# Down projections that keep sums of weights on chip, load the residual, and normalise half of the tokens around the seventh Strassen product

## The chip, the core and the metric

The kernel runs on one core of one Trainium2 chip. The core has five engines with a queue of their own each: TensorE (PE in the profile, its weight loads PEld), VectorE (DVE), ScalarE (ACT), GpSimd (POOL) and SyncE (SP). Here SP only issues DMA transfers, and so does POOL nearly always; 16 DMA engines carry them. The metric is the time of one execution on the device in microseconds (us), lower is better; a median over several runs is compared.

## What is computed

One step of a one-layer hybrid decoder for T = 1032 tokens (1024 of a prompt and 8 samples), D = 1024, all in fp32. Cut to what matters:

```
y1 = layer_norm(ALPHA * x  + 0.5 * swiglu(x,  w1_1, w3_1, w2_1))    # "ffn 1"
y2 = layer_norm(ALPHA * y1 + hybrid_mixer(y1, ...))
y  = layer_norm(ALPHA * y2 + 0.5 * swiglu(y2, w1_2, w3_2, w2_2))    # "ffn 2"

def swiglu(x, w1, w3, w2):
    return (silu(x @ w1) * (x @ w3)) @ w2        # D -> D_FF = 2816 -> D
```

The change touches only the last product of each swiglu, `@ w2`, the normalisation behind it, and the order of the first projections of the mixer behind ffn 1.

## The kernel before

Everything is held transposed: a tile is 128 features by tokens. D is 8 tiles (KD = 8, index m for outputs), D_FF is 22 (index f). Each fp32 matmul is made of three matmuls of a faster 32-bit type: an operand is split into a high part, made by ScalarE (`wh`, `gh`, `XH`), and a low part, raw minus high, made by VectorE (`wl`, `gl`, `XL`), and high x high, low x high and high x low are added up in PSUM (`mm3`, line 172). So every weight block and every operand costs a pass of ScalarE (line 91) and one of VectorE (line 94) before TensorE can use it.

**The up part** (`ffna`) makes g = -silu(x w1) (x w3) for f = 0 to 20 and stores it to DRAM: single tiles in `gs`, and for the 16 tiles f = 3 to 18 ("paired") seven operands of a Strassen scheme, `gt[P1]` to `gt[P7]`, 8 tiles of 516 tokens each (TH_ = 516 is half of the tokens, TQ = 258 a quarter; a third is 344, written `ts(t)`, NT = 3).

**The down part** (`ffnb`) has four stages:
1. `gplain(21)` computes the last tile of g on the spot, in thirds of the tokens, and leaves it split on chip. Meanwhile tile 0 is loaded back (`gload`), and VectorE rebuilds the residual `ACC = XH + XL`, 8 adds of 1032 columns. The input's tiles XH and XL are free from here on, and become the landing place of Strassen operands.
2. *Head units.* For each m and each third t, `unit` multiplies the tiles f = 0 and 21 by their weights (6 matmuls of 344 columns) and VectorE adds the result, scaled, to `ACC[:, m]`. `fill(P1, 0, m)` loads one operand tile of the first product through one of two landing buffers (`gr`) and splits it into XH and XL.
3. *Seven products* in the order P1, P5, P6, P2, P7, P4, P3. Each has four steps mp, each step two groups of 24 matmuls of 258 columns: 192 matmuls. While product o runs, the operands of product o + 1 are filled into the other slot: XH and XL hold two slots. `blocks` fetches the weight blocks of a step. P1, P2 and P4 use one block of w2 (through `wraw`, 3 buffers). P5 needs a sum of two blocks of w2, P6 that sum plus a third, P3 that one plus a fourth, P7 a sum of its own. The parts land in two halves of `rw` (4 buffers), are added on VectorE, and the running sum of P5 and P6 is stored to DRAM (`sd`, issued by POOL) and loaded again for the next product that needs it. VectorE adds PSUM into ACC, with a helper tile U for P1, P6 and P7.
4. *End units.* The tiles f = 1, 2, 19 and 20 are loaded from `gs`, and units of 12 matmuls with weights split beforehand (DRAM `hv`, fetched on POOL's queue) run chunk by chunk: three thirds in ffn 1, four quarters in ffn 2. The layer norm of a chunk (`LN`: total by a matmul with ones, line 214, mean, squares, total of squares, scale, and a new XH and XL) is a generator, `fin`, of steps set between the units of the next chunk. The last chunk's norm in ffn 1 goes on during the first projections of the mixer (`kq`, `ab`), in ffn 2 it is the tail of the kernel, with the output's stores.

The code is written in program order, and a scheduler orders the instructions on each engine; every engine then runs its own in order, and waits at semaphores. SP issues transfers in order too: one that waits for a free buffer holds up those behind it. The lines that move the sums:

```
P5: (a(1, 0), a(1, 1), 0), P6: (sd[0][mp, q], a(0, 0), 1),
P7: (a(0, 0), a(1, 0), None), P3: (sd[1][mp, q], a(0, 1), None)}[i]
...
if z is not None:
    G.dma_start(sd[z][mp, q], two[:, 0])
```

## Time and profile before

| what | value |
|---|---|
| median of 3 runs | 2562.27 us (2559.83 to 2570.35) |
| the profiled execution's own time | 2558.2 us |
| its span on the core | 2556.4 us |
| mean granted clock of TensorE | 0.991 |
| first down part: head units, products, end units | 460.53, 489.11, 658.37 to 707.70 us |
| second down part: head units, products, end units, tail | 2293.32, 2317.59, 2485.27, 2534.10 to 2556.40 us |

The stretches are cut where the first matmul of a stage starts. A row of a stretch gives its length, the busy time of each engine with the number of instructions, the granted clock, the share of the DMA engines and the traffic. Two things are read from it: a stretch with the same matmuls as another but a greater length has waits of TensorE in it (or a lower clock), and an engine whose busy time nears the length has no room for more. Which wait it was is read from the waits by engine, and what stood before it from the timeline.

### The profile page before, as it was taken

Reading aid. Unit: us, or ns where it says so; the run is one execution under the profiler, and the core shown is the slowest. Engines: PE = TensorE matmul, PEld = TensorE weight load, DVE = VectorE, ACT = ScalarE, POOL = GpSimd, SP = SyncE. Lnnn points to the kernel's source line nnn. Section 1 sums busy time; section 2 is a strip of 40 time slices with the busy share of each in tenths; the row PEclk is TensorE's granted clock in tenths of the full one; section 3 lists DMA queues with packets and bytes.
Section 4 is the critical chain, followed back from the end, with each engine's and each line's share of the span. In section 5 each row is a group of like instructions: output and inputs, shape, how many; then the busy total and the mean of one; then the engine's idle time right before and its main releaser. Section 6 shows DMA issues by size and latency. Waiting matters only on the chain.

```text
span 2556.4 us, 48972 instructions
## 1 busy us (share of the span) xinstructions
PE 2486.4 (97%) x18758; PEld 2438.4 (95%) x18758; DVE 1831.2 (72%) x3951; ACT 1168.8 (46%) x2486; POOL 435.2 (17%) x747
## 2 busy tenths in 40 slices
PE   8999999999999999999999999998999999999997
PEld 8999999999988999999999999998999999999996
DVE  7777777676797677777777686764676677777767
ACT  5433333333363746565554647633543333334336
POOL 2112121000102112111111121132521211110010
PEclk9999999999999999999999999999999999999999
DMA  6556555687411111111112111156855645447772
GB/s 231 158 178 192 166 179 167 192 269 228 117 38 54 36 48 45 39 51 34 57 35 58 35 51 37 54 159 166 231 170 146 171 137 144 133 149 228 250 208 67
DMA packets 211306, 326.43 MB, mean 128 GB/s; under 512 B 42544, under 2 KB 82992, under 8 KB 211072
## 3 DMA queue, kind: packets, MB, share of 16 engines
q1 hardware_dynamic: 143456, 192.00, 24.2%
q0 software_dynamic: 56784, 125.24, 16.8%
q10 hardware_dynamic: 10832, 6.07, 0.9%
q8 instruction: 147, 2.41, 0.4%
q14 instruction: 87, 0.71, 0.1%
HBM read 237.05 MB, written 86.18 MB: 126 GB/s over the span
## 4 chain that ended last, share of the span: by engine, by line
PE 48%; issue 20%; DMA 11%; DVE 8%; ACT 8%; POOL 5%; SPq 0%; POOLq 0%; ACTq 0%; DVEq 0%
PE ps_mm L172 29%; PE ps_g L172 5%; DMA gr<-gt 4%; ACT L91 2%; PE ps_g L1022 2%; PE ps_g L337 2%; PE ps_mm L337 2%; PE ps_sq L337 2%; DMA rw<-w 2%; POOL hv L142 2%; PE ps_sq L908 2%; DVE wl L94 1%; PE ps_g L914 1%; PE ps_g L908 1%; DMA s_S<-s 1%
## 5 line engine op out<-in xcount | busy, mean ns | idle before, releaser
L172 PE MATMUL ps_mm<-XH,wh 128*128 128x344 f32 (+1 forms) x2104 | 683.5, 325 | 5.8 <-ACT wh L91 5.7
L172 PE MATMUL ps_mm<-XH,wl 128*128 128x344 f32 (+1 forms) x2104 | 658.8, 313 | 2.0 <-DVE wl L94 2.0
L172 PE MATMUL ps_mm<-XL,wh 128*128 128x344 f32 (+1 forms) x2104 | 658.9, 313 | 0.1
L172 PEld LDWEIGHTS ps_mm<-XH,wh 128*128 128x128 f32 x2104 | 398.1, 189 | 9.6 <-ACT wh L91 5.7
L172 PEld LDWEIGHTS ps_mm<-XH,wl 128*128 128x128 f32 x2104 | 397.9, 189 | 2.8 <-DVE wl L94 2.5
L172 PEld LDWEIGHTS ps_mm<-XL,wh 128*128 128x128 f32 x2104 | 398.8, 190 | 1.7 <-DVE XL L94 0.6
L91 ACT ACTIVATE wh<-wraw 128x512 fp32r<-128x512 f32 (+1 forms) x324 | 197.8, 615 | 237.8 <-PE ps_mm L172 66.5
L94 DVE TENSOR_TENSOR wl<-wraw,wh 128x512 fp32r<-128x512 f32 (+1 forms) x324 | 218.2, 676 | 70.4 <-ACT wh L91 38.8
L337 PE MATMUL ps_g<-CH,wh 128*128 128x258 f32 x740 | 209.6, 283 | 0.6 <-DVE u L94 0.4
L337 PE MATMUL ps_g<-CH,wl 128*128 128x258 f32 x740 | 208.9, 282 | 0.0
L337 PE MATMUL ps_g<-CL,wh 128*128 128x258 f32 x740 | 208.7, 282 | 0.0
L172 PE MATMUL ps_g<-XH,wl 128*128 128x258 f32 (+1 forms) x592 | 175.1, 296 | 9.5 <-DVE wl L94 6.8
L172 PE MATMUL ps_g<-XH,wh 128*128 128x258 f32 (+1 forms) x592 | 173.1, 292 | 2.3 <-ACT wh L91 2.1
L172 PE MATMUL ps_g<-XL,wh 128*128 128x258 f32 (+1 forms) x592 | 172.5, 291 | 0.0
L337 PE MATMUL ps_mm<-XH,wl 128*128 128x258 f32 x592 | 167.0, 282 | 1.2 <-DVE wl L94 1.2
L337 PE MATMUL ps_mm<-XH,wh 128*128 128x258 f32 x592 | 167.3, 283 | 0.0
L337 PE MATMUL ps_mm<-XL,wh 128*128 128x258 f32 x592 | 166.8, 282 | 0.0
L91 ACT ACTIVATE wh<-S 128x512 fp32r<-128x512 f32 x148 | 93.1, 629 | 136.2 <-PE ps_sq L337 49.9
L91 ACT ACTIVATE XH<-gr 128x516 fp32r<-128x516 f32 x112 | 70.4, 634 | 172.5 <-DMA gr<-gt 155.9
L91 ACT ACT_TABLE_LOAD x109 | 139.8, 1283 | 6.0 <-issue 2.6
L337 PEld LDWEIGHTS ps_g<-CH,wh 128*128 128x128 f32 x740 | 139.5, 188 | 1.4 <-DVE u L94 1.2
L337 PEld LDWEIGHTS ps_g<-CL,wh 128*128 128x128 f32 x740 | 139.7, 189 | 0.0
(549 smaller groups left out, 6344.0 us busy)
## 6 DMA issues: line engine op xcount, KB each, us to landing
wraw<-w SPq DMA_DIRECT2D x164, 256.0 KB, 3.1
wraw<-w_in SPq DMA_DIRECT2D x128, 256.0 KB, 2.6
gt<-G POOLq DMA_DIRECT2D x112, 258.0 KB, 2.9
gr<-gt SPq DMA_DIRECT2D x112, 258.0 KB, 3.2
rw<-w SPq DMA_DIRECT2D x96, 256.0 KB, 4.2
wr<-w SPq DMA_DIRECT2D x76, 256.0 KB, 2.9
wh<-hv POOLq DMA_DIRECT2D x52, 256.0 KB, 3.9
wl<-hv POOLq DMA_DIRECT2D x52, 256.0 KB, 4.1
```

The lines of the kernel that those rows point to most:

```text
L91: return S.activation(out, in_, f, **kw)
L94: return (eng or V).tensor_tensor(out, a, b, op=op)
L142: G.dma_start(halves[key][i], x)
L172: PE.matmul(p, a, b, start=(n == 0), stop=(n == 3 * nk - 1))
L337: PE.matmul(ps_[c], a[:, k, :], b, start=(start and n == 0), stop=(n == 11), skip_group_check=not start)
L908: x = PE.matmul(ck(p, i), a, b, start=True, stop=True)
L914: x = PE.transpose(ck(p, i), a, IDT)
L1022: pin(PE.matmul(o[r, c, :], a(c), b(c), start=True, stop=True))
```

## The change

- The sums of weights stay on chip. Four tiles `sw` (two blocks of 512 each, in the place of g tiles) are filled with the first block for P5; the second lands in `wraw`, and VectorE adds it in place. P6 and P3 add their block to the same tile. The DRAM tensors `sd`, 16 stores and 16 loads of 256 KB in each down part, are gone. Only P7 still uses `rw`.
- The residual is loaded by 8 transfers of 528 KB from DRAM (`x` in ffn 1, `X2` in ffn 2) on SP's queue in place of 8 adds on VectorE.
- The tiles loaded from `gs` come in thirds, through the landing places s1 and lnq in place of gr, and those of the end units are asked for during P3 and P7 in place of after the last product.
- Head: tile 0 is the first of the two in the sum in place of 21; the units go (0,0), (0,1), (1,0), (1,1), (0,2), (1,2), and then by m; the fill of P1 comes behind its m's last unit. An operand tile j of a slot is now `XH[:, j, slot * 516 : ...]`, so a slot is half of the tokens of every tile.
- The products go P1, P5, P6, P3, P7, P2, P4. P4 adds only to the first half of the tokens. It is now run behind the first chunk (ffn 1) or the first two chunks (ffn 2) of the end units, which are taken from the second half of the tokens, and the norm of the chunk before it is run in steps inside it. The chunks go 2, 0, 1 in ffn 1 and 2, 3, 0, 1 in ffn 2. The weights of m = 6 and 7, which aren't held, are fetched again after P4.
- The mixer's first projections go third 2, 0, 1 in place of 0, 1, 2.

```diff
-HEAD, END = [21, 0], [1, 2, 19, 20]
+HEAD, END = [0, 21], [1, 2, 19, 20]
...
-        sd = [dr.tile([4, 2, 128, 512], F32, name="sd", tag="sd%d%d" % (n, i)) for i in range(2)]
...
             def gload(f):
                 gh, gl = gtiles()
-                for i in range(2):
-                    s = slice(i * TH_, (i + 1) * TH_)
-                    r = landing()
-                    nc.sync.dma_start(r, gs[f][:, s])
-                    split(gh[:, s], gl[:, s], r)
+                for t in range(NT):
+                    r = third(("s1", "lnq")[t % 2])
+                    nc.sync.dma_start(r, gs[f][:, ts(t)])
+                    split(gh[:, ts(t)], gl[:, ts(t)], r)
...
-                s = slice((j % 2) * TH_, (j % 2) * TH_ + TH_)
-                return [x[:, 4 * slot + j // 2, s] for x in (XH, XL)]
+                return [x[:, j, slot * TH_:(slot + 1) * TH_] for x in (XH, XL)]
...
+                if i == P5:
+                    sums.append(up.tile([128, 2, 512], F32, name="sw", tag="u", bufs=8, padded_shape=[128, 2, TH_]))
                 for q in range(2):
...
-                        two = up.tile([128, 2, 512], F32, name="rw", tag="rw", bufs=4)
-                        raw, o = (two[:, e].rearrange("p (k m) -> p k m", m=128) for e in range(2))
-                        nc.sync.dma_start(two[:, 0] if len(x.shape) == 2 else raw, x)
-                        nc.sync.dma_start(o, y)
+                        o = wp.tile([128, 4, 128], F32, name="wraw", tag="wraw", bufs=3)
+                        raw = quad(sums[mp][:, q]) if i in (P5, P6, P3) else o
+                        if i == P5:
+                            nc.sync.dma_start(raw, a(1, 0))
+                    nc.sync.dma_start(o, a(*{P1: (0, 0), P2: (0, 1), P3: (0, 1), P4: (1, 1), P5: (1, 1), P6: (0, 0), P7: (1, 0)}[i]))
+                    if raw is not o:
                         tt(raw, raw, o, OP.add)
-                        if z is not None:
-                            G.dma_start(sd[z][mp, q], two[:, 0])
...
             for m in range(KD):
-                tt(ACC[:, m, :], XH[:, m, :].bitcast(F32), XL[:, m, :].bitcast(F32), OP.add)
+                nc.sync.dma_start(ACC[:, m, :], (A["x"], X2)[n - 1][:, m, :])
             gts = [got[f] for f in HEAD]
-            for m in range(KD):
-                w = wload(w2[m][:, :2], 2)
-                fill(P1, 0, m)
-                for t in range(NT):
-                    unit(m, t, ts(t), w)
+            ws = {}
+            for m, t in [(0, 0), (0, 1), (1, 0), (1, 1), (0, 2), (1, 2)] + [(m, t) for m in range(2, KD) for t in range(NT)]:
+                if t == 0:
+                    ws[m] = wload(w2[m][:, :2], 2)
+                unit(m, t, ts(t), ws[m])
+                if t == NT - 1:
+                    fill(P1, 0, m)
...
-            order = [P1, P5, P6, P2, P7, P4, P3]
+            order = [P1, P5, P6, P3, P7, P2, P4]
...
+                    if order[o + 1:o + 2] in ([P7], [P2]):
+                        if mp % 2:
+                            got.append(gload(END[len(got)]))
+                    yield
...
+            p4 = (n, product(len(order) - 1))
             if n == 1:
-                pending = last_units(lnidx, last, [ts(t) for t in range(NT)], [up_, up_, [6, 7] + up_[:6]])
+                pending = last_units(lnidx, last, [ts(t) for t in (2, 0, 1)], [up_, up_, [6, 7] + up_[:6]], None, p4)
             else:
-                pending = last_units(lnidx, last, [slice(258 * i, 258 * i + 258) for i in range(4)], [up_] * 4, out)
+                pending = last_units(lnidx, last, [slice(TQ * i, TQ * i + TQ) for i in (2, 3, 0, 1)], [up_] * 4, out, p4)
...
+            if t == inner[0]:
+                for i, _ in enumerate(inner[1]):
+                    if i < 3:
+                        next(fin)
+                fin = None
```

Where it moves instructions, in three places. A row gives the line, the operation, the tile written and those read, and the shape; a number behind a name is that of the buffer. First, SP's queue at the head of the first down part. `gs_106` holds the stored g tiles, `gt_107` the operands of P1, `w2_1` the weights. Before:

```order
L122 DMA wraw_5812<-w3_1 128x512
L122 DMA wraw_5991<-w2_1 128x256
L122 DMA wraw_6025<-w2_1 128x256
L122 DMA wraw_6059<-w2_1 128x256
L513 DMA gr_5784<-gs_106 128x516
L513 DMA gr_5788<-gs_106 128x516
L559 DMA rw_6560<-w2_1 128x512
L560 DMA rw_6560<-w2_1 128x512
L559 DMA rw_6569<-w2_1 128x512
L560 DMA rw_6569<-w2_1 128x512
L542 DMA gr_5997<-gt_107 128x516
```

Now:

```order
L122 DMA wraw_5814<-w3_1 128x512
L511 DMA s1_5790<-gs_106 128x344
L572 DMA ACC_5779<-x 128x1032 x8
L122 DMA wraw_5993<-w2_1 128x256
L122 DMA wraw_6015<-w2_1 128x256
L539 DMA gr_6045<-gt_107 128x516
L539 DMA gr_6057<-gt_107 128x516
L122 DMA wraw_6061<-w2_1 128x256
L562 DMA sw_6562<-w2_1 128x512 x2
L562 DMA sw_6641<-w2_1 128x512
L539 DMA gr_6091<-gt_107 128x516
```

The eight loads of the residual now stand ahead of the first weights of the head, and the first fills ahead of P5's blocks.

Second, VectorE in the last product of the first down part. `ACC<-ps_g,ACC 128x258` is an eviction of a product, `wl<-wraw,wh` the low part of a weight block, `mu` and `lnq` are steps of a norm. Before, the norm's head lies between end units (evictions of 344 columns):

```order
L94 TENSOR_TENSOR s_8569<-ACC 128x344
L94 TENSOR_TENSOR ACC<-ACC,mu 128x344 x5
L94 TENSOR_TENSOR s_8577<-s_8577,lnq 128x344
L94 TENSOR_TENSOR s_8580<-s_8580,lnq 128x344
L94 TENSOR_TENSOR s_8577<-s_8577,lnq 128x344
L94 TENSOR_TENSOR ACC<-ACC,mu 128x344 x3
L94 TENSOR_TENSOR s_8580<-s_8580,lnq 128x344
L94 TENSOR_TENSOR s_8577<-s_8577,lnq 128x344
L94 TENSOR_TENSOR s_8580<-s_8580,lnq 128x344
L97 SCALAR_TENSOR_TENSOR ACC<-ps_mm,ACC 128x344
```

Now it lies in P4:

```order
L97 SCALAR_TENSOR_TENSOR ACC<-ps_mm,ACC 128x258
L94 TENSOR_TENSOR wl<-wraw,wh 128x512
L94 TENSOR_TENSOR ACC<-ACC,mu 128x344 x5
L94 TENSOR_TENSOR s_8345<-s_8345,lnq 128x344
L94 TENSOR_TENSOR s_8348<-s_8348,lnq 128x344
L94 TENSOR_TENSOR s_8345<-s_8345,lnq 128x344
L94 TENSOR_TENSOR ACC<-ACC,mu 128x344 x3
L97 SCALAR_TENSOR_TENSOR ACC<-ps_g,ACC 128x258
L94 TENSOR_TENSOR s_8348<-s_8348,lnq 128x344
L94 TENSOR_TENSOR s_8345<-s_8345,lnq 128x344
L94 TENSOR_TENSOR s_8348<-s_8348,lnq 128x344
L97 SCALAR_TENSOR_TENSOR ACC<-ps_mm,ACC 128x258
```

The steps of the norm stand on VectorE between P4's weight splits and evictions.

Third, TensorE at the very end, where the last two norms' totals (`ps_sq`, line 214) meet the last unit. Before:

```order
L172 MATMUL ps_g_30263<-gh_29593,wh_29729 128x258
L172 MATMUL ps_g_30263<-gl_29594,wh_29729 128x258
L172 MATMUL ps_g_30263<-gh_29593,wl_29730 128x258
L214 MATMUL ps_sq_30258<-s2_30154,ONES_72 128x258
L214 MATMUL ps_sq_30278<-s1_30146,ONES_72 128x258
L214 MATMUL ps_sq_30278<-ACC_26988,ONES_72 128x258 x2
```

Now:

```order
L172 MATMUL ps_mm_30240<-gh_29033,wl_30077 128x258
L214 MATMUL ps_sq_30254<-s2_30150,ONES_72 128x258
L172 MATMUL ps_g_30259<-gh_28531,wh_30095 128x258
L172 MATMUL ps_g_30259<-gl_28532,wh_30095 128x258
L172 MATMUL ps_g_30259<-gh_28531,wl_30096 128x258
L172 MATMUL ps_g_30259<-gh_28693,wh_30095 128x258
```

The older norm's total of squares (`s2`) now stands ahead of the last unit's 12 matmuls.

More of the change, by code (lines that the diff above doesn't have):

```diff
@@ L543, in fill @@
                 split(*operand(slot, j), r)
+            sums = []
             def blocks(i, mp):
@@ L578, in ffn, with product @@
             U = up.tile([128, 4, TH_], F32, name="U", tag="t")
-            order = [P1, P5, P6, P2, P7, P4, P3]
-            for o, i in enumerate(order):
+            order = [P1, P5, P6, P3, P7, P2, P4]
+            def product(o):
+                i = order[o]
                 for mp in range(4):
@@ L602, in ffn @@
                             tt(x, x, u, OP.subtract)
-            got = [gload(f) for f in END]
+                    if order[o + 1:o + 2] in ([P7], [P2]):
+                        if mp % 2:
+                            got.append(gload(END[len(got)]))
+                    yield
+            got = []
+            for o in range(len(order) - 1):
+                for _ in product(o):
+                    pass
             gts.clear()
@@ L618, in last @@
             def last(m, t, s, i):
-                if t == 0:
+                if t == 0 or m > 5 and t == n:
                     held[m] = fetch("w2%d%d" % (n, m), 1, (lambda _: hold(m)) if m < 6 else None)
@@ L635, in last_units, with last_steps @@
                 return e.value
-    def last_steps(lnidx, unit, chunks, order, out=None):
+    def last_steps(lnidx, unit, chunks, order, out=None, inner=(None, None)):
         fin = None
         for t, s in enumerate(chunks):
+            if t == inner[0]:
[3 more added lines that the diff above has]
+                fin = None
             tail = out is not None and t == len(chunks) - 1
@@ L829, in kq @@
                     evs[i][1](t, p[:, :TC])
+                kq(2, 0)
+                next(fin)
+                kq(2, 1)
+                kq(2, 2)
                 kq(0, 0)
+                next(fin)
                 next(fin)
@@ L834, in kqv_first @@
                 kq(0, 2)
+                ab(2)
+                ab(0)
+                ab(1)
                 kq(1, 0)
-                next(fin)
-                next(fin)
                 kq(1, 1)
                 kq(1, 2)
-                ab(0)
-                ab(1)
-                ab(2)
-                kq(2, 0)
-                kq(2, 1)
-                kq(2, 2)
                 gates()
```

14 lines of the change are left out of this document (7 added, 7 removed).

## The prediction

> **What bounds the kernel now.** I read the page first, for the engine that carries the span.
>
> ```profile
> span 2556.4 us, 48972 instructions
> PE 2486.4 (97%) x18758; PEld 2438.4 (95%) x18758; DVE 1831.2 (72%) x3951; ACT 1168.8 (46%) x2486; POOL 435.2 (17%) x747
> ```
>
> TensorE (PE) is busy 97% of the span. The change keeps every matmul, so it can gain only where TensorE waits or runs below full clock in the stages that it touches: the two down projections, the start of the mixer behind the first, the output behind the second. So I cut the trace at the starts of the units and products. The columns are start:end, length, busy time (and instructions) of each engine, granted clock, share of the DMA engines, GB/s. First projection: head units, then P1, P5, P6, P2, (P7, nothing lost,) P4, P3.
>
> ```profile
> core 0: us, PE busy (x) PEld busy (x) DVE busy (x) ACT busy (x) POOL busy (x), PEclk, DMA share, GB/s
> 460.53:489.11 28.58, 25.58 (x146) 25.14 (x145) 22.35 (x47) 11.54 (x22) 0.00 (x0) 0.88 0.60 170
> 489.11:512.15 23.04, 23.04 (x195) 23.04 (x193) 12.07 (x23) 9.49 (x19) 0.54 (x1) 1.00 0.54 163
> 512.15:535.28 23.13, 23.13 (x195) 23.13 (x193) 16.97 (x34) 9.76 (x17) 3.24 (x6) 1.00 0.93 307
> 535.28:559.65 24.37, 23.63 (x194) 23.18 (x193) 19.16 (x35) 8.12 (x14) 2.69 (x5) 1.00 0.91 300
> 559.65:585.26 25.61, 23.85 (x194) 23.35 (x193) 15.77 (x30) 10.30 (x18) 0.00 (x0) 1.00 0.63 194
> 608.45:634.37 25.92, 23.93 (x195) 23.32 (x194) 16.61 (x30) 9.61 (x17) 2.99 (x4) 1.00 0.77 198
> 634.37:658.37 24.00, 23.70 (x195) 23.20 (x194) 15.03 (x28) 8.84 (x14) 7.42 (x14) 1.00 0.86 252
> ```
>
> P1 is a product without a wait: 23.04 us. Against it P6 loses 1.33, P2 2.57, P4 2.88, P3 0.96, together 7.7 us. The second projection, its head units and then P6, P2, P4, P3:
>
> ```profile
> 2293.32:2317.59 24.27, 23.24 (x145) 22.68 (x145) 19.28 (x41) 10.43 (x20) 0.00 (x0) 1.00 0.64 189
> 2363.76:2388.80 25.04, 23.83 (x194) 23.21 (x193) 18.70 (x35) 8.10 (x14) 2.70 (x5) 1.00 0.91 304
> 2388.80:2413.39 24.59, 23.41 (x195) 23.20 (x193) 15.82 (x29) 10.31 (x18) 0.00 (x0) 1.00 0.66 204
> 2436.43:2461.14 24.71, 23.67 (x195) 23.25 (x194) 16.22 (x30) 9.27 (x16) 2.97 (x4) 1.00 0.75 194
> 2461.14:2485.27 24.13, 23.81 (x194) 23.21 (x193) 15.03 (x28) 9.15 (x15) 6.36 (x12) 1.00 0.85 252
> ```
>
> It loses 2.00, 1.55, 1.67 and 1.09: 6.3 us. So what can come back in the products is 14 us of 2556.
>
> **The head units.** Timelines (start, length, engine, what; in brackets the idle time before and what ended it), and three stretches:
>
> ```profile
> 440.61 5.80 DVE L94 TENSOR_TENSOR ACC<-XH,XL 128x1032 f32<-128x1032 f32 x5
> 463.23 0.63 ACT L91 ACTIVATE XH<-gr 128x516 fp32r<-128x516 f32 x1 [1.92 <-DMA gr<-gt]
> 465.04 0.49 ACT L91 ACTIVATE gh<-lnq 128x344 fp32r<-128x344 f32 x1 [0.88 <-DVE lnq L97]
> 465.59 0.66 PE L172 MATMUL ps_g<-gh,wh 128*128 128x344 f32 x1 [3.00 <-ACT gh L91]
> 445.00:455.00 10.00, 10.00 (x65) 10.00 (x65) 7.75 (x11) 2.63 (x5) 0.97 (x2) 1.00 0.88 291
> 465.00:470.00 5.00, 4.41 (x15) 4.25 (x16) 3.56 (x10) 2.12 (x5) 0.00 (x0) 0.50 0.50 139
> 770.00:775.00 5.00, 4.01 (x16) 4.01 (x17) 5.00 (x10) 1.92 (x8) 2.12 (x3) 0.68 0.27 71
> ```
>
> At full rate 65 matmuls of width 344 take 10.00 us, 0.154 each. The 146 of the first head units need 22.5 and take 28.58: 6.1 lost. Of these 3.00 are one wait: unit (0,2) needs the third chunk of tile 21, whose split comes after ScalarE has waited for a fill of P1 (its load landed at 463.23). The other 3 are the half clock after it (0.50 from 465 to 470). The second head loses 24.27 - 145 x 0.154 = 1.9.
>
> The new order runs four units (24 matmuls, 3.7 us) before the first that needs the third chunk, and the fills come behind their unit. That covers 3.00, and without the gap there is no drop. Against it stands the residual: eight loads of 528 KB, 4.23 MB, enter SP's queue between the last load of tile 0 and the head's first weights, so that w2 and P1's fills stand behind them. At the 307 GB/s of P5's row this is 13.8 us. They can start when the ACC buffer is free; the adds that they replace began at 440.61, 20 us before the first unit, so 6 us are left. But the DMA engines already carry 291 GB/s there. Some of the lateness will show: I keep 2 us of it in the first head (gain 4.0; bounds 5.9 with next to nothing late, and 6.1 - 13.8 = -7.7 with the whole transfer bare), and take -0.5 in the second, where only 1.9 can be gained (bounds 1.9 and -11.9).
>
> The load of tile 0 in thirds, through other landing buffers, leaves the two buffers of the fills alone, and the new layout lets P1's fills start when two thirds of tile 21's x are read; both are part of the same 4.0.
>
> A page's figure beside this: the Trainium skill, "DMA: Bandwidth & Descriptors", Specifications, gives about 358 GB/s from HBM to one core, by which the estimate for the residual is 11.8 us in place of 13.8; no row quoted here reaches that rate, and 307 is what I use.
>
> The removed adds (eight of 5.80/5 = 1.16 us, 9.3 us of VectorE) lie under full-rate matmuls (10.00 of 10.00 at 445 to 455): worth 0 to TensorE.
>
> **The products.** The waits between 480 and 660 (total, times, longest; TensorE's own from 535), the loads of the sums (KB each, us to landing), and VectorE's splits of the fills made during P4 (count, busy, mean ns, idle before):
>
> ```profile
> PE ps_g L172 <- DVE wl L94: 3.4, 6, 1.5
> SPq L559 <- DVE wl L94: 18.4, 17, 3.9
> ACT XH L91 <- DMA gr<-gt: 67.2, 31, 5.1
> DVE rw L94 <- DMA rw<-w: 18.2, 16, 3.4
> rw<-sd SPq DMA_DIRECT2D x32, 256.0 KB, 3.9
> L94 DVE TENSOR_TENSOR XL<-gr,XH 128x516 fp32r<-128x516 f32 x8 | 5.4, 692 | 5.9 <-ACT XH L91 5.9
> ```
>
> TensorE waits for weights split on VectorE. VectorE waits for landing weights (18.2 us), ScalarE for landing fills (67.2), and SP, which issues in order, for a free weight buffer 17 times, with the fills queued behind. Each projection stores 16 sums of 256 KB and loads them again (32 loads in two projections), 8.4 MB. After the change that is gone; at 307 GB/s it is 27 us of transfer, most of it where P5 to P3 show shares of 0.63 to 0.93. The 16 stores leave POOL's queue (POOL is busy 17%: worth 0 by itself). The second operand of P5, P6 and P3 now lands in three small buffers, and the sums' adds run as early as the sum tile allows; VectorE keeps the number of the adds, each about the 0.69 of a split of the same width, some of them pulled forward to P1 and P5, where 11 and 6 us are free in the rows above. The loads of the end tiles, in thirds, are issued earlier too: their twelve splits of 344 take 0.5 us more of VectorE than eight of 516, worth 0 while their product has VectorE time left, as P3 has 9 us. What is late next is the fill: two landing buffers, ScalarE and VectorE in order. I leave 2 us per projection for it: gains 5.7 and 4.3. Bounds: all of it (7.7 and 6.3), and 0 or 2 below it if pulled-forward adds crowd P5. I take the side near the full gain because P6 and P2, with 3.9 of the 7.7, lie on and right behind the shares of 0.93 and 0.91 that the change thins out.
>
> **The norm inside the seventh product.** VectorE's groups between 655 and 705, where one norm and the head of a second are seen, the end units as a whole, and what stands behind them:
>
> ```profile
> L94 DVE TENSOR_TENSOR ACC<-ACC,mu 128x344 f32<-128x344 f32 x16 | 7.3, 513 | 0.2 <-ACT mu L91 0.2
> L94 DVE TENSOR_TENSOR s<-s,lnq 128x344 f32<-128x344 f32 x10 | 4.6, 514 | 0.0
> L97 DVE SCALAR_TENSOR_TENSOR ACC<-ACC,LNT,s 128x344 f32<-128x344 f32 x8 | 4.2, 572 | 0.0
> L97 DVE SCALAR_TENSOR_TENSOR XL<-ACC,LNT,XH 128x344 fp32r<-128x344 f32 x8 | 4.2, 573 | 0.0
> L94 DVE TENSOR_TENSOR s<-s,ACC 128x344 f32<-128x344 f32 x12 | 6.2, 518 | 0.2
> 658.37:707.70 49.33, 47.90 (x297) 46.72 (x296) 38.09 (x83) 16.28 (x32) 4.22 (x8) 1.00 0.20 56
> 719.54 0.51 DVE L94 TENSOR_TENSOR s<-s,ACC 128x344 f32<-128x344 f32 x1
> PE ps_sq L214 <- DVE s L94: 1.4, 1, 1.4
> PE ps_mm L172 <- DVE wl L94: 2.0, 1, 2.0
> PE ps_g L908 <- DVE lt L97: 2.1, 1, 2.1
> ```
>
> One norm is 7.3/2 + 7 x 0.46 + 4.2 + 4.2 = 15.3 us of VectorE. A chunk's own eight evictions and seven sums, at 0.52 each, are 7.8, against 96 x 0.154 = 14.8 us of TensorE. P4 held 16.61 of VectorE; as the last product it has no fills to make (the 5.4 above), so 11.2 + 15.3 = 26.5 in 23.04. Queued behind a norm step on VectorE are P4's weight splits and evictions, and TensorE waits for both. The overhang of 3.5 need not all show: evictions can lag by the PSUM buffers. I take 1.5 lost in each projection, the size of the waits on a split in P2 to P4, together -3.0 (bounds 0 and -6.8).
>
> What the norm leaves elsewhere: VectorE's last sum before the mixer ran at 719.54, 12 us after the last end matmul at 707.70, and the mixer's start waits 1.4 + 2.0 + 2.1 for VectorE (from 700 to 790) and drops to 0.68 of the clock at 770 to 775. After the change two chunks stand behind P4: the first needs 3.5 + 7.8 in 14.8, so it ends clear, the second 7.8 + 15.3 in 14.8, an overhang of 8.3 in place of 12. I take the difference, 4.0 (bounds 0 and the 5.5 of waits with 1.6 of clock, 7.1). The two changed orders of its first projections ask for the chunk normed first, which is part of the same 4.0. The refetch of weights 6 and 7 (four more 256 KB loads on POOL's queue) lies under P4 and the first chunk: 0; without cover it is one transfer of 4 us.
>
> A rule to weigh: after 2 us of waiting at 770 the clock fell to 0.68 over the next 5 us, as it fell after 3.00 at 465. The Trainium skill, "TensorE: Matmul & The Clock Gate", Part 1, lets the clock fall only after an idle window of about 3.4 us; both drops here followed shorter gaps, so the trace disagrees with that as a threshold.
>
> **The tail.**
>
> ```profile
> 2534.10:2556.40 22.30, 6.24 (x18) 3.22 (x16) 13.55 (x35) 15.78 (x34) 2.91 (x4) 0.78 0.28 95
> 2540.21 0.39 ACT L91 ACTIVATE mu<-ps_sq 128x258 f32<-128x258 f32 x1
> ```
>
> The last matmul of a unit ends at 2534.1; the last norm's mean is there 6.1 us later. TensorE's order puts the older norm's second total behind the last unit before, and ahead of its 12 matmuls now; so what follows the last unit is the eviction, one add (0.5 each), the total (two matmuls of 0.12) and the mean, 2 us at the least: gain up to 4.1. But if VectorE's adds for the older total are as late as before, TensorE now waits ahead of the last unit, and little is gained. I take 2.0, the middle (bounds 0 and 4.1).
>
> **Sum.** 4.0 - 0.5 + 5.7 + 4.3 - 3.0 + 4.0 + 2.0 = 16.5. The profiled execution took 2558.2 (span 2556.4 and 1.8 around it), 4.1 below the median 2562.3 of three runs. So 2541.7 for an execution like it, 2545.8 for a median: I say 2546. All gains at their best bounds (5.9, 1.9, 7.7, 6.3, 0, 7.1, 4.1) are 33, which gives 2529; a difference of less than 0.5%, 12.8 us, a measurement can hardly tell.
>
> **Rivals.**
> - The waits stay in the products (0.22): the pair of landing buffers and the in-order splits set them. For it: ScalarE waits 67.2 us on fills, more than any engine on sums, and P2 loses 2.57 at a DMA share of 0.63. Against: fills queue behind SP's waits for weight buffers. The sum without these 10.0 is 6.5: 2556.
> - Slower (0.06): the residual stands bare at both heads, so TensorE waits L for w2 behind it and loses some 3 of clock each time: 2545.8 + 2 L + 6. Slower by 0.5% needs 2575, L = 12; the whole 13.8 gives 2579. For it: 291 GB/s already flow at 445. Against: 20 us of cover.
> - The clock falls at P4's waits (0.10): by the row at 770, a gap of 2 us costs about 5 x 0.32 = 1.6 us; two in P4, 3.2: 2549. By the Trainium skill's window (the page and part above) such gaps would cost no clock, and 2546 would stand.
> - As summed: 0.62.
>
> Faster gets 0.62 and half of the clock's case, 0.67; same the waits' 0.22 and the other half, 0.27; slower 0.06. The range reaches from 2530 to 2560, on one side the best bounds, on the other beyond the waits' case, to a residual bare for 4 us at each head.
>
> **What will show it.** Right: the first head at 24 to 26 us with clock 1.00; P6 and the products after it under 23.6; P5's and P6's DMA share well under 0.9; no sd transfers; P4 at 24 to 25 with VectorE busy nearly throughout; the mixer's waits below 3; mean within 4 us of the last matmul. Wrong: a PE wait on w2's splits at 460 and 2293; P5 or P6 with VectorE above 21 and a wait on weight splits; P4 beyond 27.

## The result, and the profile after

The changed kernel takes 2546.75 us (median of 8 runs, 2541.3 to 2553.91), the kernel before, run beside it, 2563.34 (8 runs, 2556.75 to 2570.35). The ratio is 0.9936, with a 95% interval of 0.9921 to 0.9951: 0.64% faster. Forecast were 2546 against a median of 2562.3.

The page of the profiled execution (2541.3 us, 1.8 of it around the span):

```profile
span 2539.5 us, 48802 instructions
PE 2479.7 (98%) x18758; PEld 2433.4 (96%) x18758; DVE 1814.3 (71%) x3945; ACT 1164.7 (46%) x2494; POOL 425.3 (17%) x723
```

TensorE runs the same 18758 instructions in 16.9 us less span. The stretches of the first down part, cut as those of before: head units, P1, P5, P6, P3, and P4 with the norm inside.

```profile
core 0: us, PE busy (x) PEld busy (x) DVE busy (x) ACT busy (x) POOL busy (x), PEclk, DMA share, GB/s
460.23:484.48 24.25, 23.58 (x145) 22.54 (x145) 18.46 (x39) 9.31 (x19) 0.00 (x0) 1.00 0.89 287
484.48:507.51 23.03, 23.03 (x194) 23.03 (x193) 18.88 (x37) 12.55 (x27) 0.00 (x0) 1.00 0.82 262
507.51:532.04 24.53, 23.74 (x195) 23.31 (x194) 22.20 (x44) 9.26 (x17) 0.00 (x0) 1.00 0.74 222
532.04:555.02 22.98, 22.98 (x194) 22.98 (x193) 20.92 (x39) 8.38 (x16) 0.00 (x0) 1.00 0.62 188
555.02:578.22 23.20, 23.20 (x194) 23.20 (x193) 17.25 (x33) 12.69 (x24) 0.00 (x0) 1.00 0.47 145
639.51:663.94 24.43, 24.39 (x198) 23.78 (x197) 19.41 (x42) 13.54 (x24) 2.99 (x6) 1.00 0.33 90
```

The head has its clock back (1.00 for 0.88). P6 and the products behind it, up to P4, run without a wait, and a new loss stands in P5. The second down part (head, P1, P5, P2, P4) and its only kind of wait from P1 to P5:

```profile
2280.56:2303.55 22.99, 22.99 (x146) 22.60 (x145) 18.01 (x38) 8.68 (x17) 0.00 (x0) 1.00 0.88 276
2303.55:2328.45 24.90, 23.27 (x195) 23.06 (x193) 17.66 (x34) 12.29 (x27) 0.00 (x0) 1.00 0.73 231
2328.45:2353.72 25.27, 24.17 (x194) 23.34 (x193) 22.55 (x43) 7.97 (x15) 0.00 (x0) 1.00 0.69 211
2423.81:2447.80 23.99, 23.50 (x195) 23.27 (x193) 13.15 (x25) 9.61 (x15) 5.10 (x8) 1.00 0.90 251
2471.67:2496.63 24.96, 24.32 (x198) 23.87 (x197) 18.66 (x47) 18.16 (x37) 2.12 (x4) 1.00 0.48 129
PE ps_g L172 <- DVE wl L94: 2.7, 4, 1.6
```

Here P1 and P5, which had no waits before, lose 1.9 and 2.1 (against 23.03 and 23.13) to splits that come late. P7 of this projection, 23.91 for 23.04 before, loses 0.9 too. The whole by stages, worked out from the starts of each stage's first matmul in the traces (the third column is an experiment below; the tail begins at the first total behind the last unit):

| stage, us | before | changed | sums on chip alone |
|---|---|---|---|
| up to the first head | 460.53 | 460.23 | 460.60 |
| first head units | 28.58 | 24.25 | 26.46 |
| first seven products | 169.24 | 164.36 | 164.14 |
| first end units | 48.99 | 46.51 | 48.98 |
| start of the mixer (to its first `32*32 32x32` matmul, line 1041) | 108.88 | 106.72 | 106.44 |
| middle, up to the second head | 1477.09 | 1478.50 | 1479.32 |
| second head units | 24.27 | 22.99 | 24.88 |
| second seven products | 167.68 | 169.21 | 162.61 |
| second end units | 50.72 | 47.75 | 50.71 |
| tail | 20.45 | 19.02 | 20.41 |
| span | 2556.43 | 2539.53 | 2544.56 |

The middle is the same code in every kernel, and it came out at 1476 to 1489 us in the traces. So kernels are compared below by their touched stages (all but the first row and the middle): 618.8 before, 600.8 changed. Such a sum is one execution's, and it scatters: the run with P4 as an ordinary product, below, has the changed kernel's code in P5, and there P5 takes 25.65 and 24.29 us, for 24.53 and 25.27. So about 1 us in one stage of one trace is not read as an effect. The medians beside it are of 4 to 10 runs, and their intervals are about 0.3 to 0.5% wide (8 to 13 us), so differences between two of these kernels of less than that are read from the stages alone.

### The profile page after: what moved, and what is told of

Same layout as the page of the kernel before. It is cut to its first block, busy times and chain, and to the rows that moved or that the text cites. A ratio compares the mean times of both kernels' runs of the same rounds, so it can differ in the third digit from the quotient of the medians.

```text
span 2539.5 us, 48802 instructions
## 1 busy us (share of the span) xinstructions
PE 2479.7 (98%) x18758; PEld 2433.4 (96%) x18758; DVE 1814.3 (71%) x3945; ACT 1164.7 (46%) x2494; POOL 425.3 (17%) x723
## 3 DMA queue, kind: packets, MB, share of 16 engines
q1 hardware_dynamic: 142592, 192.06, 24.4%
q0 software_dynamic: 55376, 118.95, 16.5%
## 4 chain that ended last, share of the span: by engine, by line
PE 74%; ACT 7%; DMA 7%; DVE 5%; issue 5%; POOL 2%; ACTq 0%; SPq 0%; POOLq 0%; DVEq 0%
PE ps_mm L172 33%; PE ps_g L172 9%; PE ps_mm L337 8%; PE ps_g L337 8%; PE ps_sq L337 7%; ACT L91 3%; PE ps_g L1041 2%; DMA gr<-gt 2%; PE ps_sq L927 2%; PE ps_g L927 1%; DVE wl L94 1%; PE ps_g L933 1%; ACT lnq L91 1%; DMA hv<-wl 1%; DMA s_S<-s 1%
```

## The experiments

**The sums through DRAM again.** In the changed kernel:

```diff
-                        raw = quad(sums[mp][:, q]) if i in (P5, P6, P3) else o
+                        two = up.tile([128, 2, 512], F32, name="rw", tag="rw", bufs=4)
+                        raw, o = (two[:, e].rearrange("p (k m) -> p k m", m=128) for e in range(2))
+                        nc.sync.dma_start(two[:, 0] if len(x.shape) == 2 else raw, x)
...
+                        if z is not None:
+                            G.dma_start(sd[z][mp, q], two[:, 0])
```

> The changed kernel, but the running sum of w2 blocks goes through DRAM again (stores on POOL's queue, loads on SP's, as before the change); everything else as changed. Theory: the products gained because the round trip and SP's waits for weight buffers are gone. Then P5's and P6's DMA share rises from 0.74 and 0.62 to 0.85 or more, P6 and the products after it lose 1 to 2.5 us each as they did before (P6, P3, P7, P2 stood at 22.98 to 23.20 in the first projection), and P5 is relieved (24.53 to about 23.1, its VectorE from 22.2 to 17 or 18). Net 3 to 7 us slower than the changed kernel: 2550 to 2554. Rival: the two landing buffers and the in-order splits set the waits, the place of the sums does not matter: each product within 0.5 us of the changed kernel but for P5, total within 2 us of 2546.75.

Measured: 2564.76 us, ratio to the kernel before 0.9996 (0.9978 to 1.0013): the whole gain is gone. Touched stages 616.9, 16.1 over the changed kernel, against 3 to 7 expected. P6 and P3 of the first projection:

```profile
532.29:557.41 25.12, 24.25 (x194) 23.25 (x193) 19.27 (x35) 8.23 (x15) 2.70 (x5) 1.00 0.92 303
557.41:584.22 26.81, 23.93 (x195) 23.32 (x193) 19.61 (x36) 10.74 (x19) 0.00 (x0) 1.00 0.78 249
```

The DMA share of P6 rises from 0.62 to 0.92 and its waits return. The theory had the mechanism right and the size too small. Was it the new order, with P3 right behind P6?

**The same with room between P6 and P3.**

```diff
-            order = [P1, P5, P6, P3, P7, P2, P4]
+            order = [P1, P5, P6, P2, P7, P3, P4]
```

> The changed kernel with the sums through DRAM as in the earlier run, but the products in an order that leaves the stored sums time again: P1, P5, P6, P2, P7, P3, P4 (P3 three products behind P6, not next to it). Theory: in the earlier run the 18 us came back because P3 right behind P6 loads sums that P6 has only just stored; with room, P3 falls from 26.8 to about 24 and P7 from 25 to 23.2, while P6 keeps 25 to 28: 8 to 11 us over the changed kernel by stages, a median of about 2556. Rival: the transfers themselves (8.4 MB) are the cost wherever they stand: the products lose as much in all as in the earlier run (16 us by stages), a median of about 2563.

Measured: 2568.04 us, ratio 1.0015 (0.9993 to 1.0036), touched stages 621.5. P7 fell to 22.99 as expected, but P2 rose to 27.69 and 26.71 and P3 to 30.33 and 28.20. The rival holds: the round trip costs wherever its loads stand.

**The sums on chip alone.** In the kernel before, only the sums and the order of the products are changed:

```diff
-        sd = [dr.tile([4, 2, 128, 512], F32, name="sd", tag="sd%d%d" % (n, i)) for i in range(2)]
...
+                    sums.append(up.tile([128, 2, 512], F32, name="sw", tag="u", bufs=8, padded_shape=[128, 2, TH_]))
...
-            order = [P1, P5, P6, P2, P7, P4, P3]
+            order = [P1, P5, P6, P3, P7, P2, P4]
```

> The kernel before with one part of the change alone: the sums of weights stay on chip, and the products go in the changed order (P1, P5, P6, P3, P7, P2, P4, all seven before the end units); head, residual, loads of g tiles, norms and mixer as before. Theory: the round trip of the sums set the waits from P6 on. Then P6 and the four products after it take 23.0 to 23.3 in both projections (before: 24.4, 25.6, 23.2, 25.9, 24.0 and 25.1, 24.6, 23.0, 24.7, 24.1), P5 loses 1 to 2, and the time is 8 to 12 us under before: about 2553. Rival: the changed kernel's gain in the products needs the other parts too (the end tiles' own landing places, fills that start earlier): at most 4 us under before, with waits of over 1 us left in the products behind P6.

Measured: 2548.3 us, ratio 0.9933 (0.991 to 0.9956), as fast as the changed kernel within the measurement. Its P5, P6 and P3 in the first projection and P5 in the second:

```profile
510.09:533.22 23.13, 23.13 (x194) 23.13 (x193) 20.16 (x40) 8.48 (x15) 0.00 (x0) 1.00 0.69 209
533.22:556.26 23.04, 23.04 (x194) 23.04 (x193) 21.25 (x40) 10.41 (x18) 0.00 (x0) 1.00 0.62 187
556.26:579.39 23.13, 23.13 (x194) 23.13 (x193) 15.25 (x28) 9.37 (x16) 0.00 (x0) 1.00 0.47 137
2333.88:2357.01 23.13, 23.13 (x195) 23.13 (x193) 20.54 (x40) 9.40 (x17) 0.00 (x0) 1.00 0.69 208
```

TensorE is busy in every microsecond of six products in both projections; only P4, now last, loses 2.6 and 1.1. So the sums on chip carry the gain; the smaller landing places of their blocks (`wraw` in place of `rw`) and the order of the products are part of this one step. VectorE has most of the adds of P5 and P6 in P5 here too, and P5 does not wait. What, then, does P5 wait for in the changed kernel?

**VectorE's share in it: short adds.**

```diff
-                        tt(raw, raw, o, OP.add)
+                        if i == P6:
+                            tt(raw[:, 0, :8], raw[:, 0, :8], o[:, 0, :8], OP.add)
+                        else:
+                            tt(raw, raw, o, OP.add)
```

> The changed kernel, but the 16 adds of a projection that turn P5's sums into P6's add only 8 of 512 columns of each block half (so P6's and P3's weights are not the reference's); all loads, waits and splits stay. It takes about 0.6 us from each of 8 adds on VectorE in P5 and nothing from any queue. Theory: P5 is short of VectorE (22.2 and 22.6 us busy): its busy time falls to 17 to 18, P5 from 24.5 and 25.3 to 23.0 to 23.4, total 3 us under the changed kernel. Rival: P5's weights land late (SP's queue, three weight buffers): P5 stays above 24 with VectorE at 17.

P6's sums leave out all but 8 of each block's 512 columns (8 such adds in a projection, not 16). P5 in both projections, then ScalarE's and VectorE's rows before the longest wait of TensorE in the first, 1.29 us up to 522.42:

```profile
507.27:533.27 26.00, 24.00 (x194) 23.27 (x193) 19.61 (x45) 9.14 (x17) 0.00 (x0) 1.00 0.70 212
2332.93:2359.08 26.15, 24.19 (x195) 23.37 (x193) 19.80 (x45) 9.23 (x17) 0.00 (x0) 1.00 0.71 212
521.22 0.63 ACT L91 ACTIVATE XH<-gr 128x516 fp32r<-128x516 f32 x1 [3.33 <-DMA gr<-gt]
521.76 0.61 ACT L91 ACTIVATE wh<-sw 128x512 fp32r<-128x512 f32 x1
522.40 0.69 DVE L94 TENSOR_TENSOR wl<-sw,wh 128x512 fp32r<-128x512 f32 x1 [2.09 <-ACT wh L91]
```

VectorE has over 2 us less to do, and P5 takes 1.5 and 0.9 us more (2548.88 us in all, ratio 0.993, 0.9905 to 0.9954). The theory that VectorE is short in P5 falls, and so does its rival of late weights, for this wait: the last of P5's sums was added at 511.4. ScalarE, in order, stood 3.33 us for a fill of P6 to land before it made the block's high part.

**The adds on GpSimd** (an earlier run):

```diff
-                        tt(raw, raw, o, OP.add)
+                        tt(raw, raw, o, OP.add, G if i == P6 else None)
```

> The changed kernel, but the 8 adds of each projection that make P6's sums of weights run on GpSimd (about 1.29 us each, by a like add of 128x512 in the trace) instead of VectorE. Theory: P5 waits for weight splits because VectorE carries the adds for P5 and P6 there. Then VectorE's busy time in P5 falls from 22.2 and 22.6 to about 17, P5 from 24.53 and 25.27 to 23.0 to 23.5, total 2 to 4 us faster than the changed kernel: 2543 to 2545. Rivals: the waits in P5 are late landings of weights, so P5 stays within 0.5 us; or GpSimd's adds lengthen VectorE's own operations (0.685 us now) and P5 gets longer.

Measured: 2553.22 us, ratio 0.995 (0.9924 to 0.9975); P5 26.51 and 27.43. The second rival came true. VectorE's group of weight splits in P5 (1035 ns for one, 683 in the changed kernel), and a moment of it, GpSimd's adds and two of VectorE's splits (start, length):

```profile
L94 DVE TENSOR_TENSOR wl<-sw,wh 128x512 fp32r<-128x512 f32 x8 | 8.2, 1035 | 1.5 <-ACT wh L91 1.5
513.58 4.66 POOL L94 TENSOR_TENSOR sw<-sw,wraw 128x512 f32<-128x512 f32 x3 [71.25 <-DVE XL L94]
513.63 3.47 DVE L94 TENSOR_TENSOR wl<-sw,wh 128x512 fp32r<-128x512 f32 x2
```

Two splits that take 1.3 us by themselves take 3.47 while GpSimd adds.

**The early loads of the end tiles.** First they are kept in their place in SP's queue:

```diff
-                    nc.sync.dma_start(r, gs[f][:, ts(t)])
+                    x = nc.sync.dma_start(r, gs[f][:, ts(t)])
+                    if f in END:
+                        tc.keep_in_program_order(x)
```

> The changed kernel, but the loads of the end units' g tiles keep their place in program order on SP's queue (in P3 and P7) instead of being pulled forward into P1 and P5. Theory: in the second projection P1 loses 1.85 us because a weight block stands on SP behind those loads; then P1 falls from 24.90 to 23.1 there and P5 from 25.27 to 24.5 or less, total 1 to 3 us faster than the changed kernel: 2544 to 2546. Rival: the weights are late because all transfers of P1 and P5 share the engines or because VectorE is crowded in P5 (22.2 to 22.6 us busy); P1 and P5 stay within 0.5 us, and the total with them.

P1, P5 and P2 of the second projection:

```profile
2315.36:2338.35 22.99, 22.99 (x195) 22.99 (x193) 15.53 (x29) 10.84 (x22) 0.00 (x0) 1.00 0.62 185
2338.35:2362.97 24.62, 24.02 (x195) 23.44 (x194) 22.26 (x44) 8.49 (x15) 0.00 (x0) 1.00 0.71 210
2432.37:2462.40 30.03, 25.56 (x195) 24.82 (x193) 15.84 (x29) 9.48 (x15) 5.09 (x8) 0.94 0.77 200
```

P1 comes down from 24.90 to 22.99, as expected. But in their place the loads hold P2 up by 6 us (1.1 in the first projection): 2552.47 us in all, ratio 0.9948 (0.9924 to 0.9971). Then they are issued early on GpSimd's queue:

```diff
-                    nc.sync.dma_start(r, gs[f][:, ts(t)])
+                    (G if f in END else nc.sync).dma_start(r, gs[f][:, ts(t)])
```

> The changed kernel, but the 12 loads of the end units' g tiles are issued on GpSimd's queue in place of SP's, still as early as their landing places are free. Theory: in the second projection P1 waits 1.85 us because its last weight block stands behind them on SP (pinned late, P1 came down to 22.99); off SP's queue, P1 takes 23.0 to 23.3 there, without the 6 us that the pinned loads cost in P2: total 1 to 3 us under the changed kernel, 2544 to 2546. Rival: it is the shared DMA engines, not the queue: P1 stays at 24.4 to 24.9.

P1 of the second projection:

```profile
2312.99:2337.83 24.84, 23.25 (x194) 23.04 (x193) 17.24 (x34) 12.93 (x28) 2.67 (x5) 1.00 0.67 196
```

P1 stays at 24.84 and the head before it rises to 25.13 (2549.33 us, ratio 0.9946, 0.9928 to 0.9964): the rival holds. Early loads cost P1 on either queue, so it isn't SP's order that does it. What TensorE waits for stands in the changed kernel's trace, in P1 of the second projection:

```profile
2314.53 0.63 ACT L91 ACTIVATE wh<-wraw 128x512 fp32r<-128x512 f32 x1
2321.49 0.69 DVE L94 TENSOR_TENSOR sw<-sw,wraw 128x512 f32<-128x512 f32 x1 [3.35 <-DMA wraw<-w]
2322.10 1.29 DVE L94 TENSOR_TENSOR wl<-wraw,wh 128x512 fp32r<-128x512 f32 x2
2322.84 0.39 PE L172 MATMUL ps_g<-XH,wl 128*128 128x258 f32 x1 [1.63 <-DVE wl L94]
```

The two splits at 2322.10 are those of P1's last blocks. The first block had its high part from ScalarE at 2315.16, 7 us before. But ahead of them in VectorE's order stands the add for P5's first sum, and VectorE stood 3.35 us until that sum's second block had landed. So P1's own weights were not late; a block of the next product was. The add and the two splits stand in this order in every run with the sums on chip. In the second projection the add starts 17.4 to 17.9 us after P1's first matmul in the changed kernel and in the runs with loads on GpSimd's queue, short adds, adds on GpSimd and P4 as an ordinary product, and there P1 takes 24.4 to 24.9 us. With the old head it starts after 16.4, and P1 takes 23.33; where P1 takes 22.98 to 23.04 it starts after 11.0 to 14.6. How the early loads make that block land later, by the shared transfers or by the order in which buffers come free, was not separated.

**The residual by adds, the end tiles through the fills' buffers, and both.** The two edits in the changed kernel:

```diff
-                nc.sync.dma_start(ACC[:, m, :], (A["x"], X2)[n - 1][:, m, :])
+                tt(ACC[:, m, :], XH[:, m, :].bitcast(F32), XL[:, m, :].bitcast(F32), OP.add)
```

```diff
             def gload(f):
                 gh, gl = gtiles()
+                if f in END:
+                    for i in range(2):
+                        s = slice(i * TH_, (i + 1) * TH_)
+                        r = landing()
+                        nc.sync.dma_start(r, gs[f][:, s])
+                        split(gh[:, s], gl[:, s], r)
+                    return gh, gl
```

> The changed kernel, but the residual is again made by eight adds on VectorE in place of eight loads of 528 KB. Theory: the 4.2 MB crowd the DMA engines ahead of the head (349 GB/s from 440 to 460, share 0.94, against 263 and 0.80 with the adds) and push the fills and weights of P1 and P5 back; without them P5 falls from 24.5 and 25.3 to 23.1 to 23.6, P1 in the second projection from 24.9 to under 24, the head stays within 0.5 us of 24.25 and 22.99: 2 to 4 us under the changed kernel by stages. Rival: the end tiles' loads that are pulled into P1 and P5 alone do it; then P1 and P5 stay as they are.

> The changed kernel, but the end units' g tiles land in halves in the two buffers of the fills again, so they take their turn behind the fills of P7 and P2 and can't be pulled into P1 and P5. Theory: those early loads and splits are what P1 and P5 wait behind; P1 in the second projection falls from 24.9 to 23.0 to 23.2, P5 in both to 23.1 to 23.6, and P7 and P2 pay at most 1 us for the tiles: 3 to 5 us under the changed kernel by stages. Rival: the residual's loads do it: P5 stays above 24, while P1 falls as in the run with pinned loads (22.99).

> The changed kernel with both of these undone: residual by VectorE's adds, end tiles through the buffers of the fills; kept are the sums on chip, the head's order, the norm in P4 and the mixer's order. Theory: with neither in the way every product but P4 takes 23.0 to 23.3 as in the kernel with the sums alone, the ends keep the gain of the norm in P4: by stages 4 to 7 us under the changed kernel, a median of 2540 to 2544, faster than both kernels. Rival: the head pays for the adds, or P7 and P2 for the late end tiles, and it ends within 2 us of the changed kernel.

| us | changed | adds | fill buffers | both |
|---|---|---|---|---|
| first head, second head | 24.25, 22.99 | 25.64, 24.28 | 23.76, 23.29 | 23.50, 22.67 |
| P1 of the second | 24.89 | 22.98 | 22.99 | 22.99 |
| P5, both | 24.52, 25.27 | 24.40, 23.20 | 24.11, 24.33 | 23.20, 23.20 |
| P7, both | 22.99, 23.91 | 22.99, 23.76 | 27.33, 28.15 | 25.11, 23.98 |
| P2, both | 23.20, 23.99 | 23.20, 23.94 | 23.15, 23.30 | 25.68, 24.18 |
| touched stages | 600.8 | 599.0 | 604.9 | 598.6 |
| median | 2546.75 | 2542.54 | 2547.4 | 2543.97 |
| ratio (interval) | 0.9936 (0.9921 to 0.9951) | 0.9924 (0.9905 to 0.9943) | 0.9948 (0.9932 to 0.9964) | 0.9924 (0.9908 to 0.994) |

P5 of the run with both, which has VectorE as full as the changed kernel's, and P7 of the run with the fill buffers alone:

```profile
507.11:530.30 23.19, 23.19 (x194) 23.19 (x193) 21.93 (x43) 9.65 (x17) 0.00 (x0) 1.00 0.72 217
577.62:604.94 27.32, 24.74 (x194) 24.52 (x193) 20.77 (x37) 10.53 (x18) 4.25 (x8) 0.94 0.84 257
```

Each alone misses its theory: P5 of the first projection stays at 24.40 and 24.11, and the fill buffers end 4.1 us over the changed kernel by stages, not 3 to 5 under. Only with both undone is P5 free in both projections; undoing either frees P1 of the second. So two loads that the change put early, 4.2 MB of residual and 2.1 MB of end tiles, together cost P1 and P5 their waits. They do so only beside the sums on chip: both runs with the sums through DRAM keep the two loads as early, and have 22.98 and 22.99 in P1 of the second projection and 23.20 in P5 of both. They have no add of a `sw` tile, and other buffers for P5's blocks; which of the two frees them was not tested. In turn the end tiles cost P7 4.3 and 4.2 us when they share the fills' two buffers, and P7 and P2 of the first projection 2.1 and 2.5 in the run with both; the change's own landing places avoid that. The heads are 1.4 and 1.3 us longer with the adds alone, where the expectation allowed 0.5, but shortest with both undone: no cost of the adds there is shown. Both undone is 2 us ahead of the changed kernel by stages, and about 3 by medians, with intervals that overlap: by time it can't be told from the changed kernel; from the kernel before it can. The expectation of 4 to 7 was too high, as the rival said of P7 and P2.

**The old order of the head.**

```diff
-HEAD, END = [0, 21], [1, 2, 19, 20]
+HEAD, END = [21, 0], [1, 2, 19, 20]
...
-            for m, t in [(0, 0), (0, 1), (1, 0), (1, 1), (0, 2), (1, 2)] + [(m, t) for m in range(2, KD) for t in range(NT)]:
...
+            for m in range(KD):
+                w = wload(w2[m][:, :2], 2)
+                fill(P1, 0, m)
+                for t in range(NT):
+                    unit(m, t, ts(t), w)
```

> The changed kernel with the old order of the head units (tile 21 first in the sum, m by m with the fill ahead of the units of its m). Theory: the wait of 3.0 us for the third chunk of tile 21, and the half clock after it, came from that order; the first head goes back from 24.25 to 26 to 28.5 (26.46 in the kernel with the sums alone, which has the old order too), the second from 22.99 to 24 to 25; the rest unchanged: 3 to 5 us over the changed kernel by stages. Rival: it was the new operand layout or tile 0 in thirds that freed the head: both heads within 0.7 us of the changed kernel.

The two heads:

```profile
460.50:487.52 27.02, 24.71 (x146) 24.15 (x145) 19.53 (x41) 10.47 (x20) 0.00 (x0) 0.94 0.83 263
2282.68:2308.66 25.98, 23.81 (x146) 22.67 (x145) 18.14 (x39) 9.67 (x19) 0.00 (x0) 1.00 0.79 251
```

2.8 and 3.0 us come back, with the lower clock in the first: the order freed the heads. (2546.21 us, ratio 0.9936, 0.9918 to 0.9953: by time no difference to the changed kernel.)

**P4 as an ordinary product.**

```diff
-            for o in range(len(order) - 1):
+            for o in range(len(order)):
...
-                pending = last_units(lnidx, last, [ts(t) for t in (2, 0, 1)], [up_, up_, [6, 7] + up_[:6]], None, p4)
+                pending = last_units(lnidx, last, [ts(t) for t in (2, 0, 1)], [up_, up_, [6, 7] + up_[:6]])
...
-                pending = last_units(lnidx, last, [slice(TQ * i, TQ * i + TQ) for i in (2, 3, 0, 1)], [up_] * 4, out, p4)
+                pending = last_units(lnidx, last, [slice(TQ * i, TQ * i + TQ) for i in (2, 3, 0, 1)], [up_] * 4, out)
```

> The changed kernel, but P4 is run as an ordinary seventh product and all chunks of the end units, in the changed order, behind it; the norms lie between units alone, as before the change. Theory: laying a norm into P4 took VectorE's overhang away from the mixer's start and the tail; undone, P4 takes about 23.0 (from 24.43 and 24.96), the end units and the mixer's start lose 5 to 7 us, the tail 2 to 4: net 4 to 8 us slower than the changed kernel, 2551 to 2555. Rival: what was gained there came from the earlier end tiles and the mixer's order; then within 2 us of 2546.75.

By stages: P4 22.99 and 22.98 (1.4 and 2.0 less), the end units 48.85 and 50.62 (2.3 and 2.9 more), the mixer's start 107.61 (0.9 more), the tail 21.40 (2.4 more): 5.1 us for these stages, within the 4 to 8 expected. By time 2549.12 us, ratio 0.9937 (0.9916 to 0.9958): 2.4 over the changed kernel's median, where the theory said 4 to 8 and the rival at most 2, and no difference in the ratios. That the norm in P4 gains is read from the stages of one trace and not shown by the medians.

## Why the prediction was right, and where not

The time came out 0.75 us from the forecast, and the terms do not all deserve it. Against its sum:

| term | forecast | by stages |
|---|---|---|
| first head | 4.0 | 28.58 - 24.25 = 4.3 |
| second head | -0.5 | 24.27 - 22.99 = 1.3 |
| first products | 5.7 | 169.24 - (164.36 - 1.44) = 6.3 |
| second products | 4.3 | 167.68 - (169.21 - 1.98) = 0.4 |
| norm in P4 | -3.0 | -1.44 - 1.98 = -3.4 |
| first end units and mixer | 4.0 | 2.48 + 2.16 = 4.6 |
| second end units and tail | 2.0 | 2.97 + 1.43 = 4.4 |
| not named: lead-in, middle | 0 | 0.3 - 1.4 = -1.1 |
| sum | 16.5 | 16.9 |

- *Heads: right.* The wait for the third chunk was the old order's, and the drop of the clock went with it. The lateness kept for the residual was too large in the second head. It was priced at 307 GB/s, with 20 us of cover; in the stretch ahead of the first head the loads went at

```profile
440.00:460.00 20.00, 20.00 (x129) 20.00 (x129) 6.81 (x14) 6.28 (x15) 0.55 (x1) 1.00 0.94 349
```

  349 GB/s, under matmuls at full rate. (The Trainium skill, "DMA: Bandwidth & Descriptors", Specifications, has about 358 as the limit; this row stays 3% under it and agrees.) The rival of a residual standing bare at the heads is refuted: both heads got shorter.
- *The products: the mechanism right, one term wrong.* The round trip of the sums and the waits behind it were the cause, shown from both sides (0.9996 with it restored, 0.9933 with it alone removed). Which part of the trip makes the waits, the 8.4 MB, their places in SP's order or the landing buffers `rw`, was not separated. The step that failed is "worth 0 while their product has VectorE time left": the early loads of the end tiles were priced by their splits on VectorE, and the residual only at the head. Together they cost P1 of the second projection 1.9 us and P5 1.4 and 2.1. In P1 the way is the add pulled forward onto VectorE, which the prediction had priced at nothing because VectorE has time free there: it waited 3.35 us for its block, with P1's splits behind it. "What is late next is the fill" held in P5, where a fill on ScalarE stood before the weight's high part in the run with short adds; the 2 us per projection left for it were near in size in the first projection (7.7 - 6.3 = 1.4) and too small in the second, where P7 lost 0.9 too, from a cause that no run here shows. The crowding of VectorE in P5, held there as a bound, is not what happened: with over 2 us less on it P5 did not get shorter, and at 21.93 of 23.19 busy it ran without a wait. The prediction's sign for being wrong, P5 with VectorE above 21 and a wait on splits, did come (22.2 and 22.6), and P7 and P2 of the second projection stayed above its 23.6.
- *The rival of the landing buffers (0.22)* falls for the sums: with the same two buffers six products have no wait. It is right of two other places: fills set a wait in P5, and the buffers cost P7 4 us when the end tiles use them too.
- *The norm in P4: right in size, not in kind.* Taken was the size of a wait on a split. In the first P4 TensorE was busy for 24.39 of 24.43, and had 198 instructions for 194 or so in other products: most of the loss is the totals of the norm that moved in, not a wait. VectorE had 19.41 to do and not 26.5: beside P4's own 11.2, 8.2 of the 15.3 of a norm.
- *The mixer's start: waits as forecast, the sum by chance.* 2.48 came in the end units (P4 undone gives back 2.3); 1.4 of it is the wait for the norm's total, which stood at their end before and is gone. The 2.16 behind them come out of two terms that the sum had together. The start of the mixer before, changed, and with the sums alone:

```profile
707.34:816.23 108.89, 103.51 (x665) 97.51 (x666) 100.19 (x247) 55.40 (x130) 21.03 (x32) 0.98 0.18 51
695.35:802.07 106.72, 103.49 (x664) 98.34 (x662) 95.92 (x238) 51.92 (x128) 25.09 (x34) 0.97 0.19 51
700.18:806.63 106.45, 102.32 (x666) 96.03 (x666) 99.97 (x247) 54.91 (x130) 20.95 (x32) 1.00 0.18 50
```

  TensorE's idle time in it falls from 5.4 to 3.2 us (two waits, 2.6 and 0.6, where the prediction's sign was below 3), as meant, but its clock did not come back (0.97 for 0.98). In the kernel with the sums alone the idle time falls only to 4.1, and the clock is 1.00. So the two kernels gain nearly the same by different ways. Whether the clock falls there was seen in one execution of each.
- *The tail: the mechanism right, the size too small.* In the changed kernel the older norm's total stands at 2518.64, ahead of the last unit, which ends where the last norm's first total starts, at 2520.51. The last mean is there at 2522.79, 2.3 us behind it, for 6.1 before, and TensorE did not wait ahead of the last unit, as had been feared. Two rows of TensorE, and ScalarE's, which show what stands between:

```profile
2518.64 0.60 PE L214 MATMUL ps_sq<-s,ONES 128*128 128x258 f32 x2
2520.51 0.60 PE L214 MATMUL ps_sq<-s,ONES 128*128 128x258 f32 x2
2519.27 0.48 ACT L91 ACTIVATE s<-ps_sq,EPS 128x258 f32<-128x258 f32 x1 [2.87 <-PE ps_sq L214]
2519.77 1.28 ACT L91 ACT_TABLE_LOAD   x1
2521.50 1.28 ACT L218 ACT_TABLE_LOAD   x1
2522.79 0.39 ACT L91 ACTIVATE mu<-ps_sq 128x258 f32<-128x258 f32 x1
```

  From its first work on the older norm's total to the last mean ScalarE takes 3.5 us in both kernels (2536.70 to 2540.21 before), 2.6 of it two table loads that the "2 us at the least" left out. They now lie in part under the last unit. From the last unit's end to the end of the span it is 19.0 us for 22.3, a gain of 3.3 where 2.0, the middle, was taken. In the table 1.9 of this stands under the end units, as the row of the tail begins at the total that TensorE waited for before (2534.10 to 2535.99); the other 1.1 there was not forecast.
- *The clock at P4's waits (0.10)* was not put to the test: no wait in P4 was over 1 us.

## What to carry to other kernels

A tensor that goes to DRAM only to come back one or two stages later can cost more than it looks: putting the trip back cost 16 us by stages where 3 to 7 were expected, and removing it alone gave the whole gain by time, while the other five parts of the change together gave 3.8 us by stages (604.6 to 600.8) and nothing by time. When work can go early, a load with a landing place of its own or an add that needs a block of the next product, look up where a scheduler puts it and what stands behind it on the same engine: here an add that waited 3.35 us for its block held up the splits of a product whose weights were there. And a total that comes out right proves no term: only the stages and one part at a time do.

## What the runs showed of the hardware

- *The same gap, with and without a drop of the clock.* In the kernel with the sums alone, TensorE waits at the mixer's start for the same split and as long as before the change:

```profile
763.79 0.43 PE L172 MATMUL ps_mm<-XH,wl 128*128 128x344 f32 x1 [1.96 <-DVE wl L94]
757.00:771.00 14.00, 11.95 (x80) 11.30 (x78) 13.47 (x28) 6.61 (x27) 8.04 (x9) 1.00 0.23 67
764.00:778.00 14.00, 12.04 (x71) 11.67 (x70) 13.46 (x28) 6.22 (x25) 7.28 (x7) 0.88 0.22 66
```

  The second row is its clock around that, 1.00; the third that of the kernel before around the wait at 770.99, 0.88, with 71 matmuls for 80 in as many microseconds. So the length of a gap doesn't decide. The Trainium skill, "TensorE: Matmul & The Clock Gate", Part 1, says that the window of the gate runs freely and keeps no step with the program; these two rows agree with that, though they show no window. In the changed kernel, too, the clock was 0.50 from 760 to 765, behind a wait of 2.65 us that ended at 757.47. The reading in the prediction, that a gap of 2 us brings the drop, was too simple.
- *GpSimd and VectorE hold each other up.* Two splits took 3.47 us beside GpSimd's adds, 0.68 each without. The Trainium skill, "SBUF — State Buffer", section "SBUF: two separate sides", has the two engines share a pair of ports under a lock that one holds for a whole instruction, also for a VectorE instruction with two SBUF inputs beside a GpSimd one that reads SBUF; the rows above agree. Moving an add from a full VectorE to GpSimd, busy 17% of the span, made the stage 2 us longer. That is not all by the lock: SP also waited 12.4 us there for buffers that GpSimd's slower adds held (1.43 us each).
